# Second matmul in seven block products, x cast in DRAM and turned by DMA, row checks moved: a gated MLP on one Trainium2 core

## The chip, the core and the metric

The kernel runs on one core of one Trainium2 chip. The metric is device time in microseconds (us), so less is better. A time is the median of several executions; a profile is one execution taken by the hardware profiler, and its span is 1.6 to 1.9 us shorter than the time of that execution. PE is the tensor engine (TensorE), PEld its weight load, DVE VectorE, ACT ScalarE, POOL GpSimd, SP SyncE.

## The reference

```python
batch, seq, dim, hidden = 16, 256, 512, 2048
x:  [16, 256, 512]   w1: [512, 4096]   w2: [2048, 512]      # float32, normal draws
h = x @ w1
gate, value = np.split(h, 2, axis=-1)
h = np.maximum(gate, 0) * value
return (h @ w2).astype(np.float32)
```

## The kernel before

The 4096 rows of x are four superblocks (s = 0 to 3 in the code, one to four in the text) of 1024 rows. In each, a first matmul makes 16 hidden blocks of 128 columns, by a Strassen-Winograd scheme: the 2x2 block product of (two row halves of x) x (two halves of the contraction) with (gate, value) takes seven products P1 to P7 in place of eight, on sums of x (S1 to S4) and of w1 (T1 to T4) that are made beforehand. Each product here is two matmuls of 512 columns. Then the second matmul, h times w2, is done plainly.

```python
SLOT = {"P1": 0, "P5": 1, "P2": 3, "P6": 4, "P3": 5, "P7": 9, "P4": 13}   # in steps; a block has a period of 7

class Block:                                    # one hidden block of the first matmul
    def P1(self):
        self.X = psx.tile(...); self.mm("P1", self.X, True)
        self.Y = psy.tile(...); nc.scalar.copy(out=self.Y, in_=self.X)          # ScalarE, PSUM to PSUM
    def P5(self):
        self.W = psw.tile(...); self.mm("P5", self.W, True)
        nc.scalar.activation(self.p5, self.W, COPY, scale=GS)                   # ScalarE
    def P2(self):
        self.mm("P2", self.X, False)            # adds to X: must wait for the copy of X to Y
    def P6(self):
        self.mm("P6", self.Y, False)
        nc.scalar.activation(self.u2, self.Y, COPY, scale=GS)                   # ScalarE
    def P3(self): ...                           # two VectorE instructions
    def P7(self): ...                           # one
    def P4(self): ...                           # one: writes the second half of g

def mm2_stream(s, g):                           # the second matmul: 8 x 16 matmuls of 512 columns
    for b in range(NB):
        ps = psx.tile([P, DO], F32, name="O", tag="X")
        for hc in range(NJ):
            nc.tensor.matmul(ps, g[:, hc, b * P:(b + 1) * P], w2_sb[:, hc, :], start=hc == 0, stop=hc == NJ - 1)
            ...
        nc.scalar.activation(o, ps, COPY, scale=1 / GS)                         # ScalarE evicts
        nc.sync.dma_start(out=out_v[s, b], in_=o)

def look_whole(t, at, of, half=False):          # a row check: sum of squares, on ScalarE
    nc.scalar.activation(sq[:, :of], t, SQUARE, scale=..., accum_out=st[:, at:at + 1])

# which block of which superblock gets a check behind its P6
LOOKS = {(1, i): lambda i=i: look_w1(i) for i in range(16)}
LOOKS.update({(0, 8 + i): lambda i=i: look_first(i) for i in range(8)})
LOOKS.update({(2, i): lambda i=i: look_w2(i) for i in range(8)})
```

The checks decide on the device whether the inputs fit the scaled fp16 way; if not, a general fallback runs. x is loaded in 32-row strips, cast by ScalarE and transposed by VectorE during the second matmul. Each engine works through its own instructions in order.

## Time and profile before

| | before |
|---|---|
| time, median (range) | 336.24 us (336.1 to 336.59, 4 runs) |
| span of the profile, granted clock | 334.7 us, 0.997 |
| superblocks one to four | 72.3, 79.7, 78.3, 77.7 us |
| start to the first block / last matmul to the end | 20.8 / 5.9 us |

A superblock is timed here from its first block's first matmul to that of the next superblock, read in the PE timeline. Below are, from the page of the kernel before, the busy time of each engine and the busy tenths of PE and ACT in 40 equal slices of the span.

```profile
PE 321.7 (96%) x1475; PEld 145.0 (43%) x1475; DVE 199.5 (60%) x307; ACT 180.6 (54%) x332; POOL 113.1 (34%) x142
PE   8979999999999999999999999999999999999992
ACT  2568798832267878764128785554215555541120
```

PE is busy 96%, so it sets the time; but a busy PE can still be stretched. The timeline of the kernel before shows what a matmul costs. Columns are start, length, engine, line, operation, output and inputs, shape and count; in brackets is idle time and its releaser.

```profile
6.75 1.69 PE L148 MATMUL X<-warm 128*128 128x256 f16 x14
...
99.15 0.60 ACT L242 ACTIVATE pu<-Y 128x512 f32<-128x512 f32 x1 [0.59 <-PE Y L221]
99.64 1.05 ACT L173 ACTIVATE sq<-w_B_88 128x1024 f16<-128x1024 f16 x1
99.81 0.59 PE L221 MATMUL X<-x_A_782,w_B_88 128*128 128x512 f16 x2
100.59 0.19 ACT L173 ACTIVATION_READ_ACCUMULATOR sq<-w_B_88 128x1 f32 x1
100.68 0.59 PE L221 MATMUL Y<-x_S_788,w_T_93 128*128 128x512 f16 x2
100.68 0.59 ACT L228 COPY Y<-X 128x512 f32<-128x512 f32 x1
101.32 0.59 PE L221 MATMUL X<-x_A_783,w_B_89 128*128 128x512 f16 x2
```

The warm-up line prices a 256-column matmul, weight load included: 14 take 1.69 us and the last lasts 272 ns, so they start (1.69 - 0.272) / 13 = 0.109 us apart. The other lines are one block of superblock two. Products start 0.43 us apart, so P2, on w_B_89, should start at 101.11. It starts at 101.32, because it must wait for the copy of X to Y (L228), which began at 100.68 although its X, P1 of 99.81, was complete some 0.3 us before. ScalarE was still in the row check (L173) and its read-out. I call such a delay a hole: the step from one matmul's start to the next, less 0.2158 us (512 columns) or 0.1092 us (256). Superblock two has holes of 3.7 us in all, three of 2.2, one of 3.0 (1.5 and 0.64 of them in its first two blocks), four none to speak of.

### The profile page before, as it was taken

The page shows a single profiled execution, that of the slowest core. Times are in us where ns is not written, and L with a number is a line of the kernel's source. Part 1 is how long each engine was busy: PE and PEld are TensorE (multiplying, and loading weights), DVE is VectorE, ACT ScalarE, POOL GpSimd, SP SyncE. Part 2 cuts the span into 40 slices and gives each one's busy share as a digit, 9 for nine tenths or more (in the row PEclk, how much of TensorE's full clock was granted, in tenths as well). Part 3 has the DMA queues.
Part 4 walks back from the last instruction along what each step waited for, and adds up shares of the span by engine and source line. Part 5 has one row for each costly group of instructions (what it writes and reads, how often), then busy time and mean ns, then how long its engine had stood idle before and what let it go on. Part 6 is the DMA issues. An engine that isn't in the chain of part 4 may idle for free. (4 is left out here: it accounts for less than half of the span.)

```text
span 334.7 us, 4222 instructions
## 1 busy us (share of the span) xinstructions
PE 321.7 (96%) x1475; PEld 145.0 (43%) x1475; DVE 199.5 (60%) x307; ACT 180.6 (54%) x332; POOL 113.1 (34%) x142
## 2 busy tenths in 40 slices
PE   8979999999999999999999999999999999999992
PEld 4634444444444444444443444444444444444441
DVE  0477888866038778775207788885805888882000
ACT  2568798832267878764128785554215555541120
POOL 1679979299800000038950000019970000000000
PEclk9999999999999999999999999999999999999998
DMA  8946599942126000004116300004120000000212
GB/s 252 358 144 182 195 238 161 169 113 78 63 90 163 1 0 0 2 1 158 65 63 162 58 2 0 0 2 125 63 96 31 1 1 2 0 0 33 94 65 69
DMA packets 30458, 27.59 MB, mean 82 GB/s; under 512 B 1632, under 2 KB 25440, under 8 KB 30432
## 3 DMA queue, kind: packets, MB, share of 16 engines
q1 hardware_dynamic: 27136, 24.52, 24.8%
q0 software_dynamic: 2112, 2.10, 3.9%
q10 hardware_dynamic: 1184, 0.66, 0.6%
q8 instruction: 13, 0.21, 0.3%
q14 instruction: 13, 0.11, 0.1%
HBM read 20.97 MB, written 8.39 MB: 88 GB/s over the span
## 5 line engine op out<-in xcount | busy, mean ns | idle before, releaser
L286 PE MATMUL O<-w_sb,g 128*128 128x512 f16 x512 | 113.4, 379 | 0.0
L248 DVE SCALAR_TENSOR_TENSOR cc<-W,pu 128x512 f32<-128x512 f32 x62 | 42.9, 692 | 73.3 <-ACT pu L242 73.2
L286 PEld LDWEIGHTS <-g 128*128 128x128 f16 x512 | 50.1, 98 | 60.5 <-issue 0.2
L164 POOL TENSOR_TENSOR fold<-xh 128x1024 f32<-128x1024 f16 x12 | 24.0, 1999 | 114.0 <-ACT xh L186 113.3
L298 ACT ACTIVATE o<-O 128x512 f32<-128x512 f32 x31 | 18.5, 597 | 69.1 <-PE O L286 65.3
L242 ACT ACTIVATE pu<-Y 128x512 f32<-128x512 f32 x62 | 37.0, 597 | 33.6 <-PE Y L221 32.7
L228 ACT COPY Y<-X 128x512 f32<-128x512 f32 x62 | 35.9, 578 | 25.1 <-PE X L221 17.9
L249 DVE SCALAR_TENSOR_TENSOR g<-X,cc 128x512 f16<-128x512 f32 x62 | 42.9, 692 | 2.3
L258 DVE SCALAR_TENSOR_TENSOR g<-Y,cc 128x512 f16<-128x512 f32 x62 | 42.3, 681 | 2.7 <-PE Y L221 2.7
L167 POOL TENSOR_TENSOR fold<-fold 128x512 f32<-128x512 f32 (+2 forms) x72 | 41.3, 574 | 5.6
L254 DVE SCALAR_TENSOR_TENSOR cc<-Y,pu 128x512 f32<-128x512 f32 x62 | 42.3, 682 | 0.1
L235 ACT ACTIVATE pu<-W 128x512 f32<-128x512 f32 x62 | 37.1, 598 | 0.0
L221 PEld LDWEIGHTS <-w_B_89 128*128 128x128 f16 x124 | 12.1, 97 | 23.3 <-issue 12.0
L221 PEld LDWEIGHTS <-w_T_94 128*128 128x128 f16 x124 | 12.1, 97 | 15.8 <-issue 3.5
L221 PEld LDWEIGHTS <-w_T_93 128*128 128x128 f16 x124 | 12.1, 98 | 14.6
L221 PEld LDWEIGHTS <-w_T_91 128*128 128x128 f16 x124 | 12.1, 98 | 14.6
L221 PEld LDWEIGHTS <-w_B_88 128*128 128x128 f16 x124 | 12.0, 97 | 14.7
L221 PEld LDWEIGHTS <-w_T_92 128*128 128x128 f16 x124 | 12.0, 97 | 14.7
L221 PEld LDWEIGHTS <-w_B_90 128*128 128x128 f16 x124 | 12.0, 98 | 14.4
L295 DVE TENSOR_SCALAR o<-O 128x256 f32<-128x256 f32 x1 | 0.4, 425 | 25.3 <-ACT o L293 25.3
L186 ACT CAST xh<-xs 128x1024 f16<-128x1024 f32 x12 | 12.2, 1042 | 5.4 <-DMA xs<-in_x_dram 5.4
L203 POOL TENSOR_TENSOR w_T_91<-w_stage 128x512 f16<-128x512 f32 x7 | 9.2, 1313 | 7.5 <-DMA w_stage<-in_w_dram 7.3
(155 smaller groups left out, 429.9 us busy)
## 6 DMA issues: line engine op xcount, KB each, us to landing
out_dram<-o SPq DMA_DIRECT2D x31, 256.0 KB, 2.0
w_stage<-in_w_dram SPq DMA_DIRECT2D x7, 1024.0 KB, 6.9
xs<-in_x_dram SPq DMA_DIRECT2D x48, 128.0 KB, 3.9
w_sb<-in_w_dram POOLq DMA_DIRECT2D x4, 512.0 KB, 8.6
w_stage<-in_w_dram ACTq DMA_DIRECT2D x1, 512.0 KB, 5.3
w_stage<-in_w_dram SPq DMA_DIRECT2D x1, 512.0 KB, 6.6
x_A_162<-in_x_dram SPq DMA_DIRECT2D x1, 256.0 KB, 2.8
x_A_163<-in_x_dram SPq DMA_DIRECT2D x1, 256.0 KB, 4.1
```

Source lines behind the costliest of these rows:

```text
L164: nc.gpsimd.tensor_tensor(fold, t, t, op=MULT)
L167: nc.gpsimd.tensor_tensor(fold[:, :, :m], fold[:, :, :m], fold[:, :, m:2 * m], op=ADD)
L221: nc.tensor.matmul(ps, wop[wn][:, b, self.jb * P:(self.jb + 1) * P], self.xo[xn][:, b, :], start=fresh and b == 0, stop=b == 1, skip_group ...
L228: nc.scalar.copy(out=self.Y, in_=self.X)
L235: nc.scalar.activation(self.p5, self.W, COPY, scale=GS)
L242: nc.scalar.activation(self.u2, self.Y, COPY, scale=GS)
L248: nc.vector.scalar_tensor_tensor(out=self.c12, in0=self.W, scalar=GS, in1=self.u2, op0=MULT, op1=ADD)
L249: nc.vector.scalar_tensor_tensor(out=self.g[:, self.jb, :TH], in0=self.X, scalar=0.0, in1=self.c12, op0=MAX, op1=MULT)
L254: nc.vector.scalar_tensor_tensor(out=self.c22, in0=self.Y, scalar=GS, in1=self.p5, op0=MULT, op1=ADD)
L258: nc.vector.scalar_tensor_tensor(out=self.g[:, self.jb, TH:], in0=self.Y, scalar=0.0, in1=self.c22, op0=MAX, op1=MULT)
L286: nc.tensor.matmul(ps, g[:, hc, b * P:(b + 1) * P], w2_sb[:, hc, :], start=hc == 0, stop=hc == NJ - 1)
L298: nc.scalar.activation(o, ps, COPY, scale=1 / GS)
```

## The change

Its intent: the second matmul goes through the same seven products, on 128-row pairs of tokens with 256 output columns, so 7/8 of the work. To free ScalarE and VectorE for it, x of later superblocks is cast to fp16 by a DMA from DRAM to DRAM, turned by DMA transposes, and the sums of x for superblocks three and four go to GpSimd in the first matmul (those for superblock two stay on VectorE, the checks of later x on GpSimd as before). The checks of w1 and w2 move into the second matmul. One more difference is not in the cut below: each load of w1 for two blocks, 1 MB before, is now two of 512 KB. The diff, cut to its core:

```diff
-    w2_sb = wpool.tile([P, NJ, DO], F16, name="w2_sb")
+    vop = {n: wpool.tile([P, NJ // 2, DO // 2], F16, name=f"v_{n}") for n in ("B11", "B21", "B22", "T1", ... "T4")}
-    def turn_x(o, t, i): ...          # ScalarE cast, VectorE transposes
+    def cast_x(s):
+        x16[s] = dram.tile([2 * TH, D], F16, name="x16")
+        nc.gpsimd.dma_start(out=x16[s], in_=x2[s * 2 * TH:(s + 1) * 2 * TH, :])
+    def load_x(s, o):
+        for h in range(2):
+            for e in range(4):
+                nc.sync.dma_start(out=o[f"A{h + 1}{e // 2 + 1}"][:, e % 2],
+                                  in_=x16[s][h * TH:(h + 1) * TH, e * P:(e + 1) * P], transpose=True)
...
-    def mm2_stream(s, g): ...
+    class Pair:                       # 7 products of 8 matmuls with 256 columns
+        def P1(self): ... nc.scalar.copy(out=self.Y, in_=self.X)
+        def P5(self): nc.scalar.activation(self.pu[:, 0], self.W, COPY, scale=1 / GS); some_look()
+        def P2(self): nc.scalar.activation(self.o[:, 0, :DO // 2], self.X, COPY, scale=1 / GS)
+        def P6(self): nc.scalar.activation(self.pu[:, 1], self.Y, COPY, scale=1 / GS); some_look()
+        def P3(self): nc.vector.scalar_tensor_tensor(...)      # W + pu[1]
+        def P7(self): nc.vector.scalar_tensor_tensor(...)      # Y + pu[0]
+        def P4(self): nc.scalar.activation(...)
+    ORDER = ("P1 0, P1 1, P2 0, P2 1, P5 0, P6 0, P3 0, P7 0, P5 1, P4 0, P6 1, P3 1, P7 1, P1 2, P4 1, P5 2, P2 2, "
+             "P6 2, P3 2, P7 2, P1 3, P4 2, P5 3, P2 3, P6 3, P3 3, P7 3, P4 3")
...
-    LOOKS = {(1, i): lambda i=i: look_w1(i) for i in range(16)}
-    LOOKS.update({(0, 8 + i): lambda i=i: look_first(i) for i in range(8)})
-    LOOKS.update({(2, i): lambda i=i: look_w2(i) for i in range(8)})
+    LOOKS = {(0, 2 + i): lambda i=i: look_first(i) for i in range(8)}
+    LOOK_JOBS = [... look_w1(i), 16 ...] + [... look_w2(i), 8 ...]     # taken by some_look, 8 in each of s = 0, 1, 2
+    CASTS = {(0, 7): 1, (0, 13): 2, (1, 3): 3}                         # (superblock, block): which x is cast
+    SUMS_AT = (10, 11, 12, 13), (22, 26, 34, 38), (46, 53, 57, 61), (70, 78, 82, 87)   # VectorE, S1 S2 S4 S3 of each pair
...
+                    elif todo == len(wl):                              # at block 12 of superblock one
+                        for n2, i0, i1 in (("T1", "T3", "B11"), ("T2", "B22", "T1")):
+                            nc.gpsimd.tensor_tensor(vop[n2], vop[i0], vop[i1], op=SUB)
+                    if 4 <= todo < 8:                                  # a quarter of w2, cast as it is loaded
+                        nc.gpsimd.dma_start(out=vop[n2], in_=w2_v[...])
+        if s == 0:
+            job(20, lambda: nc.vector.tensor_tensor(vop["T3"], vop["B22"], vop["T3"], op=SUB))
+            job(30, lambda: nc.vector.tensor_tensor(vop["T4"], vop["B21"], vop["T2"], op=SUB))
```

"P7 0" is product P7 of pair 0; the text calls the pairs first to fourth. A product has four steps of two matmuls, and a job at step n is recorded on its engine just before that step's matmuls.

More of the change, by code (lines that the diff above doesn't have):

```diff
@@ L116, in fast_way @@
     gpool = ctx.enter_context(tc.tile_pool(name="gpool", bufs=1))
-    stage = ctx.enter_context(tc.tile_pool(name="stage", bufs=3))
+    dram = ctx.enter_context(tc.tile_pool(name="dram", bufs=NS - 1, space=bass.MemoryType.DRAM))
     halfs = ctx.enter_context(tc.tile_pool(name="halfs", bufs=4))
@@ L122, in fast_way @@
     psw = ctx.enter_context(tc.tile_pool(name="psw", bufs=2, space=bass.MemoryType.PSUM))
-    x_v = x2.rearrange("(s h tb r) (q c) -> s h q r tb c", h=2, tb=16, r=32, q=4)
-    w1_v = w1.rearrange("(p e) (g j) -> p (e g) j", e=4, g=2)
-    w2_v = w2.rearrange("(hc p) n -> p hc n", p=P)
-    out_v = out2.rearrange("(s b p) n -> s b p n", p=P, b=NB)
+    w1_v = w1.rearrange("(e p) (g j) -> g p e j", p=P, g=2)
+    w2_v = w2.rearrange("(u hc p) (v n) -> u v p hc n", u=2, v=2, p=P)
+    out_v = out2.rearrange("(s h b p) n -> s h b p n", p=P, h=2, b=NB // 2)
     wop = {n: wpool.tile([P, 2, H], F16, name=f"w_{n}") for n in ("B11", "B21", "B22", "T1", "T2", "T3", "T4")}
-    w2_sb = wpool.tile([P, NJ, DO], F16, name="w2_sb")
+    vop = {n: wpool.tile([P, NJ // 2, DO // 2], F16, name=f"v_{n}") for n in ("B11", "B21", "B22", "T1", "T2", "T3", "T4")}
     w_stage = wpool.tile([P, 4, 1024], F32, name="w_stage")
@@ L151, in x_tiles, with sums_of @@
     def x_tiles():
-        return {n: xpool.tile([P, 2, TH], F16, name=f"x_{n}", tag=f"x_{n}")
-                for n in ("A11", "A12", "A21", "A22", "S1", "S2", "S3", "S4")}
-    def x_sums(o):
+        o = {n: xpool.tile([P, 2, TH], F16, name=f"x_{n}", tag=f"x_{n}")
+             for n in ("A11", "A12", "A22", "S1", "S2", "S3", "S4")}
+        o["A21"] = o["S3"]
+        return o
+    def sums_of(o, eng=nc.vector):
         for n, i0, i1, op in (("S1", "A21", "A22", ADD), ("S2", "S1", "A11", SUB), ("S4", "A12", "S2", SUB),
                               ("S3", "A11", "A21", SUB)):
-            yield nc.vector.tensor_tensor(o[n], o[i0], o[i1], op=op)
+            yield eng.tensor_tensor(o[n], o[i0], o[i1], op=op)
     def look(t, at):
@@ L174, in look_whole, with load_rows @@
                              accum_out=st[:, at:at + 1])
-    def load_x(s, i):
-        t = stage.tile([P, 8, P], F32, name="xs", tag="xs")
-        for q in range(4):
-            nc.sync.dma_start(out=t[q * 32:(q + 1) * 32], in_=x_v[s, i // 2, q, :, i % 2 * 8:i % 2 * 8 + 8])
-        return t
-    def turn_x(o, t, i):
-        ts = slice(i % 2 * 256, i % 2 * 256 + 256)
-        c = halfs.tile([P, 8, P], F16, name="xh", tag="xh")
-        nc.scalar.copy(out=c, in_=t)
-        halves.append(c)
-        for k in range(2):
-            nc.vector.transpose(o[f"A{i // 2 + 1}{k + 1}"][:, :, ts].rearrange("p b (tb r) -> p b tb r", r=32),
-                                c.rearrange("p tb (c k b) -> p k b tb c", k=2, b=2)[:, k])
+    x16 = {}
+    def cast_x(s):
[6 more added lines that the diff above has]
+                                  in_=x16[s][h * TH:(h + 1) * TH, e * P:(e + 1) * P], transpose=True)
+    def load_rows(s, i):
+        t = halfs.tile([P, 8, P], F16, name="xh", tag="xh")
+        nc.sync.dma_start(out=t.rearrange("p (b q) c -> p b (q c)", b=2),
+                          in_=x16[s][i * 2 * P:(i + 1) * 2 * P].rearrange("(b p) d -> p b d", p=P))
+        return t
     def load_w1(eng, jb, n, u):
-        t = w_stage[:, u:u + n].rearrange("p u v -> p (u v)").rearrange("p (eg j) -> p eg j", eg=8)
-        eng.dma_start(out=t, in_=w1_v[:, :, jb * P:(jb + n) * P])
-        return t.rearrange("p (k b g) j -> p k b g j", k=2, b=2)
+        t = w_stage[:, u:u + n].rearrange("p u v -> p (u v)").rearrange("p (g e j) -> p g e j", g=2, e=4)
+        for v in range(2):
+            eng.dma_start(out=t[:, v], in_=w1_v[v, :, :, jb * P:(jb + n) * P])
+        return t.rearrange("p g (k b) j -> p k b g j", k=2)
     def w1_ops(jb, n, t):
@@ L279, in products @@
                                            in1=v, op0=MAX, op1=MULT)
-    def mm2_stream(s, g):
-        last = s == NS - 1
-        for b in range(NB):
-            ps = psx.tile([P, DO], F32, name="O", tag="X")
-            for hc in range(NJ):
-                nc.tensor.matmul(ps, g[:, hc, b * P:(b + 1) * P], w2_sb[:, hc, :],
-                                 start=hc == 0, stop=hc == NJ - 1)
-                if hc < NJ - 1:
-                    yield
-            o = tmp.tile([P, DO], F32, name="o", tag="tmp")
-            if last and b == NB - 1:
-                h = DO // 2
-                nc.scalar.activation(o[:, :h], ps[:, :h], COPY, scale=1 / GS)
-                nc.scalar.dma_start(out=out_v[s, b, :, :h], in_=o[:, :h])
-                nc.vector.tensor_scalar(out=o[:, h:], in0=ps[:, h:], scalar1=1 / GS, scalar2=None, op0=MULT)
-                nc.sync.dma_start(out=out_v[s, b, :, h:], in_=o[:, h:])
-            else:
-                nc.scalar.activation(o, ps, COPY, scale=1 / GS)
-                nc.sync.dma_start(out=out_v[s, b], in_=o)
-            yield
@@ L302, in advance, with __init__, product, send @@
-    def advance(stream, n):
+    s_place = w_stage.rearrange("p u v -> p (u v)").bitcast(F16).rearrange("p (i n h t) -> p i n h t", i=2, n=4, t=P)
+    class Pair:
+        def __init__(self, s, g, t):
+            self.s, self.t = s, t
+            self.end = s == NS - 1 and t == NB // 2 - 1
+            o = {f"A{h + 1}{u + 1}": g[:, u * NJ // 2:(u + 1) * NJ // 2, h * TH + t * P:h * TH + (t + 1) * P]
+                 for h in range(2) for u in range(2)}
+            o.update({f"S{n + 1}": s_place[:, t % 2, n] for n in range(4)})
+            self.op = o
+        def product(self, name):
+            c = slice(0, DO // 2)
+            if name == "P1":
+                self.X = psx.tile([P, TH], F32, name="X", tag="X")[:, c]
+            elif name == "P5":
+                self.W = psw.tile([P, TH], F32, name="W", tag="W")[:, c]
+            ps = self.X if name in ("P1", "P2") else self.W if name in ("P5", "P3") else self.Y
+            wn, an = WX[name]
+            for i in range(NJ // 2):
+                nc.tensor.matmul(ps, self.op[an][:, i], vop[wn][:, i], start=name in ("P1", "P5") and i == 0,
+                                 stop=i == NJ // 2 - 1, skip_group_check=True)
+                if i == NJ // 2 - 1:
+                    getattr(self, name)()
+                if i % 2:
+                    yield
+        def send(self, h, c):
+            nc.sync.dma_start(out=out_v[self.s, h, self.t, :, c], in_=self.o[:, h, c])
+        def P1(self):
+            self.Y = psy.tile([P, TH], F32, name="Y", tag="Y")[:, :DO // 2]
+            nc.scalar.copy(out=self.Y, in_=self.X)
+        def P5(self):
+            self.pu = tmp.tile([P, 2, DO // 2], F32, name="pu2", tag="tmp")
+            nc.scalar.activation(self.pu[:, 0], self.W, COPY, scale=1 / GS)
+            some_look()
+        def P2(self):
+            self.o = tmp.tile([P, 2, DO], F32, name="o", tag="tmp")
+            nc.scalar.activation(self.o[:, 0, :DO // 2], self.X, COPY, scale=1 / GS)
+        def P6(self):
+            nc.scalar.activation(self.pu[:, 1], self.Y, COPY, scale=1 / GS)
+            some_look()
+        def P3(self):
+            nc.vector.scalar_tensor_tensor(out=self.o[:, 0, DO // 2:], in0=self.W, scalar=1 / GS, in1=self.pu[:, 1],
+                                           op0=MULT, op1=ADD)
+            self.send(0, slice(0, DO))
+        def P7(self):
+            nc.vector.scalar_tensor_tensor(out=self.o[:, 1, DO // 2:], in0=self.Y, scalar=1 / GS, in1=self.pu[:, 0],
+                                           op0=MULT, op1=ADD)
+            if self.end:
+                self.send(1, slice(DO // 2, DO))
+        def P4(self):
+            nc.scalar.activation(self.o[:, 1, :DO // 2], self.Y, COPY, scale=1 / GS)
+            self.send(1, slice(0, DO // 2 if self.end else DO))
@@ new lines, in fast_way, with mm2_stream @@
+    ORDER = ("P1 0, P1 1, P2 0, P2 1, P5 0, P6 0, P3 0, P7 0, P5 1, P4 0, P6 1, P3 1, P7 1, P1 2, P4 1, P5 2, P2 2, "
+             "P6 2, P3 2, P7 2, P1 3, P4 2, P5 3, P2 3, P6 3, P3 3, P7 3, P4 3")
+    LAST_ORDER = ORDER.replace("P1 3, P4 2, P5 3, P2 3, P6 3, P3 3, P7 3", "P1 3, P5 3, P2 3, P6 3, P4 2, P7 3, P3 3")
+    def mm2_stream(s, pairs):
+        for step in (LAST_ORDER if s == NS - 1 else ORDER).split(", "):
+            name, t = step.split()
+            yield from pairs[int(t)].product(name)
@@ L303, in advance @@
+    stream_at = {}
+    def advance(stream, n, todo={}):
         for _ in range(n):
-            if stream is None or next(stream, 0) == 0:
+            if stream is None:
                 return
+            at = stream_at[stream] = stream_at.get(stream, -1) + 1
+            for job in todo.get(at, ()):
+                job()
+            next(stream, 0)
     wl = [(0, 1, 0), (1, 1, 1)] + [(jb, 2, jb % 4) for jb in range(2, NJ, 2)]
@@ L345, in fast_way @@
     x_nat = x2.rearrange("(s h b p) d -> s h b p d", h=2, b=4, p=P)
-    place = list(x_tiles().values())
-    xn = [[t.rearrange("p b t -> p (b t)").bitcast(F32) for t in place[4 * h:4 * h + 4]] for h in range(2)]
+    place = [*x_tiles().values()][:7] + [halfs.tile([P, 8, P], F16, name="xh", tag="xh")]
+    xn = [[t.rearrange("p a b -> p (a b)").bitcast(F32) for t in place[4 * h:4 * h + 4]] for h in range(2)]
     def fetch_first(h):
@@ L357, in turn_first @@
             for e in range(4):
-                nc.tensor.transpose(ps[:, e * P:(e + 1) * P], xn[h][b].rearrange("p (c e) -> p e c", e=4)[:, e], ident)
+                nc.tensor.transpose(ps[:, e * P:(e + 1) * P], xn[h][b][:, e * P:(e + 1) * P], ident)
             for k, copy in ((0, nc.vector.tensor_copy), (1, nc.scalar.copy)):
@@ L383, in fast_way @@
     prepare(3)
-    sums = x_sums(xo)
+    sums = sums_of(xo)
     next(sums)
@@ L392, in fast_way, with some_look @@
     copy_some(2)
-    halves, LOOKX = [], {}
+    LOOKX, looks = {}, []
+    def some_look():
+        if looks:
+            looks.pop(0)()
     def look_x(s, i):
-        look(halves[i], 32 * s - 24 + 8 * i)
-        if i == 3:
-            halves.clear()
+        look(load_rows(s, i), 32 * s - 24 + 8 * i)
     def look_w1(i):
@@ L408, in look_w2 @@
     def look_w2(i):
-        look_whole(w2_sb[:, 2 * i:2 * i + 2].rearrange("p h n -> p (h n)"), NX + 16 + i, 1024)
+        n = ("B11", "B21", "B22", "T1")[i // 2]
+        look_whole(vop[n].rearrange("p (u h) n -> p u (h n)", u=2)[:, i % 2], NX + 16 + i, 1024, n == "T1")
     def judge():
@@ L428, in fast_way @@
         LOOKX.update({(s, 2 * i): (s, i) for i in range(4)})
-    LOOKS = {(1, i): lambda i=i: look_w1(i) for i in range(16)}
-    LOOKS.update({(0, 8 + i): lambda i=i: look_first(i) for i in range(8)})
-    LOOKS.update({(2, i): lambda i=i: look_w2(i) for i in range(8)})
+    LOOKS = {(0, 2 + i): lambda i=i: look_first(i) for i in range(8)}
+    LOOK_JOBS = [lambda i=i: look_w1(i) for i in range(16)] + [lambda i=i: look_w2(i) for i in range(8)]
     LOOKS[3, 10] = judge
@@ L436, in fast_way @@
     TAIL = 4
+    CASTS = {(0, 7): 1, (0, 13): 2, (1, 3): 3}
+    SUMS = (9, 10, 11, 12)
+    SUMS_AT = (10, 11, 12, 13), (22, 26, 34, 38), (46, 53, 57, 61), (70, 78, 82, 87)
     for s in range(NS):
@@ L444, in fast_way @@
         stream = None
-        if s + 1 < NS:
-            xs = []
         last = NJ * PERIOD
@@ L450, in fast_way @@
             if at == last - 7:
-                stream = mm2_stream(s, g)
+                pairs = [Pair(s, g, t) for t in range(NB // 2)]
+                stream = mm2_stream(s, pairs)
             if at in plan:
@@ L459, in fast_way @@
                     elif todo == len(wl):
-                        for h0 in (0, 4, 8, 12):
-                            nc.gpsimd.dma_start(out=w2_sb[:, h0:h0 + 4, :], in_=w2_v[:, h0:h0 + 4, :])
+                        for n2, i0, i1 in (("T1", "T3", "B11"), ("T2", "B22", "T1")):
+                            nc.gpsimd.tensor_tensor(vop[n2], vop[i0], vop[i1], op=SUB)
                         for j in range(0, NPLAIN, 2):
                             plain_w_end(j, 2)
-                if n == "P1" and jb in (9, 11, 13) and s + 1 < NS:
-                    xs.append(load_x(s + 1, len(xs)))
+                    if 4 <= todo < 8:
+                        n2 = ("B11", "T3", "B22", "B21")[todo - 4]
+                        nc.gpsimd.dma_start(out=vop[n2], in_=w2_v[(0, 0, 1, 1)[todo - 4], (0, 1, 1, 0)[todo - 4]])
+                if n == "P1" and jb == (10 if s == 0 else 1) and s + 1 < NS:
+                    xo_next = x_tiles()
+                    load_x(s + 1, xo_next)
+                if n == "P1" and (s, jb) in CASTS:
+                    cast_x(CASTS[s, jb])
+                if s and n == "P3" and jb in SUMS and s + 1 < NS:
+                    if jb == SUMS[0]:
+                        sums = sums_of(xo_next, nc.gpsimd)
+                    next(sums)
                 getattr(blocks[jb], n)()
@@ L476, in fast_way, with job @@
                 advance(prev, 2)
-        if s + 1 < NS:
-            xo = x_tiles()
-            turn_x(xo, xs[0], 0)
-            advance(stream, 6)
-            turn_x(xo, xs[1], 1)
-            xs.append(load_x(s + 1, 3))
-            advance(stream, 12)
-            turn_x(xo, xs[2], 2)
-            advance(stream, 18)
-            turn_x(xo, xs[3], 3)
-            for _ in x_sums(xo):
-                pass
-            advance(stream, NB * NJ - TAIL - 46)
+        jobs = {}
+        def job(at, *what):
+            jobs.setdefault(at, []).extend(what)
+        for t, at in enumerate(SUMS_AT):
+            sums = sums_of(pairs[t].op)
+            for u in at:
+                job(u, lambda sums=sums: next(sums))
+        if s == 0:
+            job(20, lambda: nc.vector.tensor_tensor(vop["T3"], vop["B22"], vop["T3"], op=SUB))
+            job(30, lambda: nc.vector.tensor_tensor(vop["T4"], vop["B21"], vop["T2"], op=SUB))
+        if s + 1 < NS:
+            xo = xo_next
+            if s == 0:
+                sums = sums_of(xo)
+                for u in (84, 90, 93, 96):
+                    job(u, lambda sums=sums: next(sums))
+            looks = [lambda i=i: LOOK_JOBS[i]() for i in range(8 * s, 8 * s + 8)]
+            advance(stream, 112 - TAIL - 10, jobs)
         else:
@@ L492, in fast_way @@
                                    skip_runtime_bounds_check_because="a comparison wrote it")
-            advance(stream, NB * NJ)
+            advance(stream, 112, jobs)
         prev = stream
```

## The prediction

> **What bounds the kernel now.** TensorE. The page gives PE 96% of the 334.7 us span, and a granted clock of 0.997. In the timeline two 512-column matmuls start every 0.431 us: 215.8 ns each; 900 of the first matmul and 512 of the second make 304.7 us. The rest is start (first real matmul at 11.0 us), end (6 us after the last matmul), and holes. In the PE timeline, start to start beyond the nominal step, I count 3.0 us in superblock one's first matmul (1.5 and 0.64 in its first two blocks), 3.7 us in superblock two, 2.2 in three. The last two are regular: 0.21 us per block, always before the product that needs X copied to Y, and only where ScalarE also does a 128x1024 row check of w1 or w2 (1.05 + 0.19 us): ScalarE is the slower engine there. Superblock four has neither.
>
> **What the change removes.**
> 1. The second matmul goes from 128 matmuls of 512 columns to 224 of 256 per superblock. The trace prices them: the 14 warm-up matmuls 128x256, each with its weight load, take 1.69 us in the timeline, the last 272 ns, so 109 ns start to start. This agrees with the Trainium skill, "TensorE: Matmul & The Clock Gate", Back-to-back issue gap (N/2.4 + 2.5 ns). 224 x 0.1092 = 24.5 us against 27.6: 12.6 us in all, on the critical path.
> 2. The w1 and w2 checks move from ScalarE in the first matmul into the second, where it is 30% busy: 5.9 us of holes go.
> 3. ScalarE's casts (12.2 us) and VectorE's transposes (16 us) of x leave; they were hidden, but make room for the sums.
>
> **What it adds.**
> - 64 VectorE sums of 128x1024 fp16, 0.69 us each where GpSimd is quiet: 11 us per 24.5 us stage, hidden except the first: after the last block's g write (0.6 us) S1 needs 0.69, and only 1.3 us of products stand between: 0.25 us per stage.
> - ScalarE checks between evictions: P7 of the first pair waits for P6's eviction behind a check, 0.2 us per stage; output buffers in a rotation of four: some tenths more.
> - Superblock one: x checks move onto blocks 2 to 9, where weight casts also load ScalarE (+0.6 us); w2 loads (4 MB, cast) run beside the w1 loads, whose landing (6.9 us) has about 2 us of room: 0 to 4 us, 1.5 expected; T3 on VectorE delays P7 0, 0.3 us.
> - DRAM casts and DMA transposes: off the path. GpSimd sums and checks within the first matmul: free, as VectorE's PSUM operations kept 0.69 us beside GpSimd's weight sums.
>
> Sum: 336.3 - 12.6 - 5.9 + 4.2 = 322.
>
> **Predicted: 322 us, range 318.5 to 327.5. Faster by over 2%: 0.94; within 2%: 0.05; slower: 0.01.**
>
> **What would show each step.** Second-matmul stages of 24.5 to 25.5 us; no 0.21 us holes in superblocks two and three; superblock one's holes at 3 to 7 us, ended by ScalarE or a w1 DMA; second-matmul holes ended by VectorE sums (before P5 of pair 0) and ScalarE evictions. Start and end unchanged within 0.5 us.
>
> **What would make it wrong.** 256-column matmuls not hiding real weight loads; w2 or cast traffic starving w1; GpSimd slowing VectorE's fp16 sums (up to 2.4 us beside GpSimd in this trace); DMA transposes so slow that superblock two starts late; ScalarE blocked on output buffers, rippling into the products.

## The result, and the profile after

The changed kernel takes 325.21 us (322.68 to 325.93, 4 runs) against 336.24 us. The ratio is 0.9657 (0.9604 to 0.9709): faster. A ratio here is the mean time of one kernel's fast runs over that of the other's in the same rounds, so not quite the ratio of the medians quoted.

The prediction's range held it, 3.2 us above the 322 predicted. The kernel before keeps within about half a microsecond in those runs; the changed one spreads over 3.2 us. In the longest later series, 11 runs of the kernel before spread over 1.75 us and 6 of the changed one over 3.1. Page of the changed kernel:

```profile
PE 307.2 (95%) x1859; PEld 181.6 (56%) x1859; DVE 229.0 (71%) x372; ACT 181.3 (56%) x368; POOL 135.6 (42%) x155
PE   8979998997999999999999999999999999999992
ACT  2569996435665555545766555545665555552230
```

Next, busy time of each engine by superblock, before and then after. Columns: window, length, busy us (instructions started) of PE, PEld, DVE, ACT, POOL, then the granted clock, DMA share and GB/s.

```profile
20.78:93.07 72.29, 70.09 (x321) 31.23 (x320) 49.13 (x72) 45.47 (x87) 57.70 (x62) 1.00 0.63 153
93.07:172.74 79.67, 78.42 (x354) 34.30 (x353) 49.13 (x76) 50.83 (x92) 22.89 (x32) 1.00 0.18 54
172.74:251.05 78.31, 77.41 (x353) 34.34 (x352) 52.19 (x76) 43.13 (x76) 22.81 (x32) 1.00 0.19 54
251.05:328.79 77.74, 77.74 (x358) 34.63 (x356) 42.13 (x69) 31.62 (x56) 0.00 (x0) 1.00 0.08 28
```

```profile
20.82:95.04 74.22, 67.89 (x414) 40.02 (x412) 57.35 (x89) 52.28 (x111) 44.64 (x34) 1.00 0.69 155
95.04:168.73 73.69, 73.40 (x450) 43.62 (x448) 54.69 (x88) 42.32 (x84) 30.29 (x37) 1.00 0.26 72
168.73:242.42 73.69, 73.40 (x450) 43.61 (x448) 54.70 (x88) 42.33 (x84) 29.77 (x36) 1.00 0.19 58
242.42:317.18 74.76, 74.62 (x459) 44.34 (x456) 55.80 (x94) 34.47 (x68) 21.33 (x32) 1.00 0.13 45
```

Superblock two is 5.98 us shorter, three 4.62, four 2.98. Superblock four had no checks before and prepares no later x, so its gain is that of the seven products: 3.16 us on paper, less a hole of 0.30. The other two add their checks' holes. But superblock one became 1.9 us longer: PE is busy 67.9 of 74.2 us there, and its holes went from 3.0 to 8.1 us. Holes in the changed kernel's PE timeline, as I count them:

| where | us | predicted |
|---|---|---|
| one, first matmul, blocks 2 and 3 (there before: 2.14) | 2.23 | as before |
| one, blocks 4 to 9, before P2, ScalarE casts and x checks (there before: 0.88, in part other blocks) | 1.14 | +0.6 |
| one, blocks 11 and 12 | 2.17 | 1.5 (w1 loads) |
| one, second matmul, before P5 of the first pair | 0.60 | 0.25 |
| one, before P7 of the first pair | 0.62 | 0.5 |
| one, before P4 of the first pair | 1.36 | none |
| two and three, before P5 of the first pair | 0.37 and 0.36 | 0.25 each |
| two and three, before P7 of the first pair | 0.25 and 0.25 | 0.2 each |
| four, before P5 of the first pair | 0.30 | 0.25 |

The hole at blocks 11 and 12, in the timeline of the changed kernel (superblock one, end of the w1 loads):

```profile
54.07 0.60 PE L230 MATMUL W<-x_S_196,w_T_90 128*128 128x512 f16 x2
54.65 0.62 ACT L216 CAST w_B_89<-w_stage 128x512 f16<-128x512 f32 x1 [2.31 <-DMA w_stage<-in_w_dram]
54.77 1.25 POOL L212 TENSOR_TENSOR w_T_90<-w_stage 128x512 f16<-128x512 f32 x1 [4.99 <-DMA w_stage<-in_w_dram]
55.17 0.59 ACT L251 ACTIVATE pu<-Y 128x512 f32<-128x512 f32 x1
55.81 0.59 PE L230 MATMUL Y<-x_S_198,w_T_92 128*128 128x512 f16 x2 [1.14 <-ACT pu L251]
```

The DMA times of the w1 loads, from the kernel's instructions on their staging tile, before and then after:

```profile
DMA to landing us min/median/max: 5.3/6.6/8.9
```

```profile
DMA to landing us min/median/max: 3.8/5.7/13.1
```

ScalarE and GpSimd wait 2.31 and 4.99 us for the last piece of w1. ScalarE's cast of that piece stands in order before the eviction of Y (L251), and P7 waits for that: PE stands still. The slowest w1 load, of 512 KB, took 13.1 us to land; before, of 1 MB, it was 8.9.

The hole before P4 of the first pair, in the same kernel's timeline:

```profile
77.08 1.04 PE L312 MATMUL W<-v_T_97,w_stage 128*128 128x256 f16 x8
77.39 0.42 DVE L340 SCALAR_TENSOR_TENSOR o<-W,pu_845 128x256 f32<-128x256 f32 x1
77.72 1.22 DVE L571 TENSOR_TENSOR v_T_100<-v_B_95,v_T_98 128x2048 f16<-128x2048 f16 x1
78.86 0.41 DVE L345 SCALAR_TENSOR_TENSOR o<-Y,pu_845 128x256 f32<-128x256 f32 x1
79.32 0.93 PE L312 MATMUL Y<-v_T_100,g 128*128 128x256 f16 x7 [1.20 <-DVE o L345]
```

P5 of the second pair starts at 77.08, and P4 of the first should follow at 77.95. P4 adds to Y, which VectorE must first have read for P7 (L345). VectorE does so at 78.86 only: T4 (L571), 128x2048, was placed one step ahead of it. P4 also multiplies by T4, so it needs both. From 72.03 until both are done VectorE is never idle for more than 0.1 us: it has too much to do before P4.

### The profile page after: what moved, and what is told of

The parts are those of the page before. It is cut to its first block, busy times and chain, and to the rows that moved or that the text cites. A ratio compares the mean times of both kernels' runs of the same rounds, so it can differ in the third digit from the quotient of the medians.

```text
span 323.5 us, 5169 instructions
## 1 busy us (share of the span) xinstructions
PE 307.2 (95%) x1859; PEld 181.6 (56%) x1859; DVE 229.0 (71%) x372; ACT 181.3 (56%) x368; POOL 135.6 (42%) x155
## 4 chain that ended last, share of the span: by engine, by line
PE 86%; DVE 5%; ACT 5%; issue 2%; DVEq 0%; ACTq 0%
PE Y L230 24%; PE X L230 16%; PE W L230 15%; PE Y L312 12%; PE W L312 7%; PE X L312 7%; PE Y L148 2%; DVE w_stage L161 2%; ACT sq L176 1%; PE X L283 1%; PE W L283 1%; DVE g L267 1%; ACT Y L237 1%; ACT w_B_88 L216 1%; DVE x_A_193 L428 1%
## 5 line engine op out<-in xcount | busy, mean ns | idle before, releaser
L167 POOL TENSOR_TENSOR fold<-xh 128x1024 f32<-128x1024 f16 x12 | 22.7, 1894 | 107.9 <-DMA xh<-x_704 40.9
L251 ACT ACTIVATE pu<-Y 128x512 f32<-128x512 f32 x62 | 37.0, 597 | 34.6 <-PE Y L230 33.8
L312 PEld LDWEIGHTS <-w_stage 128*128 128x128 f16 x512 | 49.7, 98 | 9.0 <-DVE w_stage L161 2.1
L312 PEld LDWEIGHTS <-g 128*128 128x128 f16 x384 | 37.5, 98 | 9.7 <-issue 1.6
L170 POOL TENSOR_TENSOR fold<-fold 128x512 f32<-128x512 f32 (+2 forms) x72 | 38.8, 539 | 5.6
L161 DVE TENSOR_TENSOR w_stage<-g 128x1024 f16<-128x1024 f16 x32 | 21.2, 690 | 0.2
L312 PE MATMUL Y<-v_T_100,g 128*128 128x256 f16 x128 | 17.1, 272 | 1.2 <-DVE o L345 1.2
L312 PE MATMUL W<-v_T_97,w_stage 128*128 128x256 f16 x128 | 16.6, 273 | 1.0 <-DVE w_stage L161 0.8
L312 PE MATMUL Y<-v_T_99,w_stage 128*128 128x256 f16 x128 | 16.6, 273 | 0.6 <-DVE v_T_99 L570 0.5
```

What stands on the lines that cost most here:

```text
L161: yield eng.tensor_tensor(o[n], o[i0], o[i1], op=op)
L167: nc.gpsimd.tensor_tensor(fold, t, t, op=MULT)
L170: nc.gpsimd.tensor_tensor(fold[:, :, :m], fold[:, :, :m], fold[:, :, m:2 * m], op=ADD)
L312: nc.tensor.matmul(ps, self.op[an][:, i], vop[wn][:, i], start=name in ("P1", "P5") and i == 0, stop=i == NJ // 2 - 1, skip_group_check=True)
```

## The experiments

Ten kernels ran, all with correct results, against runs of the kernel before on the same chip (335.4 to 337.2 us). The series were taken on three chips; the kernel before had medians of 336.12, 336.25 and 336.25 us there, so times are compared across them. Their lengths of superblocks and holes are read in the PE timelines as above.

### 1. The changed kernel again

No edit.

> The changed kernel once more, unedited: a base for the other runs and a look at its own spread (322.7 to 325.9 us so far, where the kernel before keeps within 0.5 us). Theory 'cast': superblock one has a hole of about 2.2 us at blocks 11 and 12, where ScalarE and GpSimd wait for the last w1 load, and whether that load loses the race against the DRAM cast of x differs from run to run; so runs lie from 322.5 to 326 us. Rival 'w2': the four cast loads of w2 share the DMA engines with w1 and always slow it by the same; then the hole is there in every run and the spread has another source. Expected median 324.5 to 325.5.

Measured: 325.36 us (322.87 to 325.95, 6 runs), ratio 0.967. One run of six took 322.9 us, as one of the first four took 322.7; the others lie near 325. The profiled run was one of the longer ones; the hole at blocks 11 and 12 was there with 1.07 us, and its size thus differs between runs (2.17 in the first profile). Experiments 4 to 7 leave the program up to there as it is, and give four more profiles. Ordered by the landing of the slowest w1 load, 10.5, 10.6, 12.3, 12.5, 12.7 and 13.1 us, the six have holes of 0, 0.26, 1.31, 1.53, 1.07 and 2.17 us.

### 2. The first cast of x later

```diff
-    CASTS = {(0, 7): 1, (0, 13): 2, (1, 3): 3}
+    CASTS = {(0, 11): 1, (0, 13): 2, (1, 3): 3}
-                if n == "P1" and jb == (10 if s == 0 else 1) and s + 1 < NS:     # load_x: the DMA transposes
+                if n == "P1" and jb == (12 if s == 0 else 1) and s + 1 < NS:
```

> The first DRAM cast of x is issued at block 11 instead of 7, which in GpSimd's order is after the last w1 load has landed; its DMA transposes start at block 12 and have until the end of the stage. Theory 'cast': the wait for the last w1 load at blocks 11 and 12 goes, 1.5 to 2.2 us less than the unedited run's median, 322.5 to 323.3, and the spread of the runs falls to about 1 us. Rival 'w2': the hole stays, time within 0.5 us of the unedited run. If the transposes then come too late, a new hole stands at the start of superblock two or before the sums of x on VectorE late in stage one.

Measured: 323.11 us (322.13 to 324.18, 5 runs), ratio 0.9621 (0.9597 to 0.9644). The hole is gone, superblock one is 71.9 us long, and the slowest w1 load lands in 9.1 us. The four loads of w2 were untouched, so the rival falls. The hole was absent in one profile with the cast in its place too, so the time counts here more than the one profile; and the transposes moved with the cast, which experiment 3 leaves alone. The spread only fell to 2 us: part of it is elsewhere (the first block starts between 20.4 and 21.7 us in the profiles of kernels with the same start).

### 3. The casts cut into rows, in their places

```diff
-        nc.gpsimd.dma_start(out=x16[s], in_=x2[s * 2 * TH:(s + 1) * 2 * TH, :])
+        rows = "(b p) d -> p b d"
+        nc.gpsimd.dma_start(out=x16[s].rearrange(rows, p=P),
+                            in_=x2[s * 2 * TH:(s + 1) * 2 * TH, :].rearrange(rows, p=P))
```

> The casts keep their places, but each is cut into 1024 rows of 2 KB read and 1 KB written, spread over 128 outer steps[...]. Theory 'cast by large packets': the w1 load's last packets and its semaphore no longer stand behind packets of 16 to 32 KB, so the wait at blocks 11 and 12 falls from 2.3 us to under 1 us although the same bytes move at the same time; time 322.5 to 324. Rival 'bytes': what matters is that 3 MB more move beside the load, whatever the packet size; then the hole stays at 1.5 to 2.5 us and the time within 0.5 us of the unedited run. Rival 'w2': no change either.

Measured: 322.83 us (321.96 to 323.72, 4 runs), ratio 0.9598 (0.9577 to 0.9619). The hole is gone though the same bytes move at the same time. Windows of two us, first the changed kernel, whose last w1 load lands at 54.62, then the one with rows, where it lands at 50.11 (columns as above):

```profile
50.00:52.00 2.00, 2.00 (x11) 0.90 (x10) 1.55 (x4) 1.77 (x4) 0.00 (x0) 1.00 1.02 217
52.00:54.00 2.00, 2.00 (x11) 0.89 (x10) 1.16 (x2) 0.33 (x1) 0.00 (x0) 1.00 0.39 83
```

```profile
50.00:52.00 2.00, 2.00 (x10) 0.87 (x9) 1.56 (x3) 1.64 (x4) 1.74 (x3) 1.00 1.26 209
52.00:54.00 2.00, 2.00 (x11) 0.93 (x10) 1.55 (x4) 1.74 (x4) 2.00 (x3) 1.00 1.24 208
```

Its w1 loads:

```profile
DMA to landing us min/median/max: 3.9/5.7/8.3
```

In the changed kernel GpSimd does nothing in these 4 us and ScalarE almost nothing in the last two. The DMA figures need care: these windows count a packet where it starts, with its whole length. Spread over the time that the packets take, the records give 217 and 216 GB/s and a DMA share of 1.01 in both windows, so the engines were full, and the bytes moved as fast as with rows (207 and 209, counted in the same way).

What differs is how the end of the load fits in. The cast has 32 packets of 32 KB and 2.43 us: 16 start from 49.0 to 50.3, as many as there are engines, the other 16 from 51.4 to 52.7, each as one of the first ends. Of the w1 load's queue 2 data packets (1 KB and 0.06 us) were left at 49.45. They start at 51.67 and 51.76, between the two rounds, and two packets of 4 bytes, the last before the landing, at 54.14 and 54.23, as the second round ends. So the last of the load waits one or two packets of 2.43 us. The landings agree: where the queue is through between the rounds, the load lands at 52.1 and 52.2 us (the profiles with holes of 0 and 0.26), otherwise at 54.3 to 54.6.

With rows of 1 KB the load lands in 8.3 us at worst, and GpSimd goes on working. The Trainium skill, "DMA: Bandwidth & Descriptors", Queues, rings and completion order, says that each DMA engine takes turns between queues packet by packet. That fits these times. The packet records don't say which engine a packet is on, so they don't show the turns of one engine by themselves.

### 4. T4 on GpSimd

```diff
-                        for n2, i0, i1 in (("T1", "T3", "B11"), ("T2", "B22", "T1")):
+                        for n2, i0, i1 in (("T1", "T3", "B11"), ("T2", "B22", "T1"), ("T4", "B21", "T2")):
-            job(30, lambda: nc.vector.tensor_tensor(vop["T4"], vop["B21"], vop["T2"], op=SUB))
```

> The sum T4 of w2 (128x2048) is made by GpSimd straight after T2 instead of by VectorE at step 30 of the first second matmul. Theory 'T4': the 1.36 us hole before the first pair's P4 is P4 waiting for VectorE's read of Y, which stands behind T4 in VectorE's order; it goes, and the time falls by 1.2 to 1.4 us. Rival 'contention': GpSimd, now busy 4 us longer, slows the first fp16 sums on VectorE (0.87 us and more in place of 0.69), and the hole before the first pair's P5 grows from 0.60 us by as much as is won; time within 0.5 us of the unedited run.

Measured: 327.85 us (324.84 to 328.61, 6 runs), ratio 0.9769: 2.5 us slower than the unedited kernel. The hole before P4 fell to 0.24 us, but those before P5, P6, P3 and P7 of the first pair became 1.35, 0.68, 0.68 and 0.85. VectorE and GpSimd in its timeline:

```profile
70.65 1.62 DVE L161 TENSOR_TENSOR w_stage<-g 128x1024 f16<-128x1024 f16 x1
71.69 1.60 POOL L408 TENSOR_TENSOR w_T<-w_B,w_T 128x512 f16<-128x512 f16 x1
72.37 1.47 DVE L161 TENSOR_TENSOR w_stage<-w_stage,g 128x1024 f16<-128x1024 f16 x1
73.25 1.60 POOL L409 TENSOR_TENSOR w_T<-w_B,w_T 128x512 f16<-128x512 f16 x1
73.87 1.53 DVE L161 TENSOR_TENSOR w_stage<-g,w_stage 128x1024 f16<-128x1024 f16 x1
75.32 0.68 DVE L161 TENSOR_TENSOR w_stage<-g 128x1024 f16<-128x1024 f16 x1
```

VectorE's fp16 sums took 1.47 to 1.62 us in place of 0.69 while GpSimd worked on its own sums, which are pushed 4 us later by T4, and the sum at 75.32, after GpSimd's last, took 0.68 again. The rival was right, and stronger than I had it. The Trainium skill, "SBUF — State Buffer", Who interferes with whom, says that a VectorE instruction with two SBUF inputs contends with a GpSimd instruction that reads SBUF, and one with at most one SBUF input, outside the two-port modes, does not. This agrees on both: VectorE's operations on PSUM in the first matmul kept 0.69 us beside GpSimd's weight sums. All these holes together are 1.2 us more than the unedited kernel's in the same place; its profiled run took 326.08 us, where four of the six took 327.8 to 328.6. That profile has no hole at blocks 11 and 12, where the unedited kernel's have 1.07 and 2.17; the longer runs probably had one, which would make up most of the rest, but no profile of them shows it.

### 5. T4 after the read, on VectorE

```diff
-            job(30, lambda: nc.vector.tensor_tensor(vop["T4"], ...
+            job(32, lambda: nc.vector.tensor_tensor(vop["T4"], ...
-    ORDER = ("... P7 0, P5 1, P4 0, P6 1, P3 1, ...
+    ORDER = ("... P7 0, P5 1, P6 1, P4 0, P3 1, ...
```

> T4 stays on VectorE but comes after VectorE's read of Y for P7 of the first pair, and P4 of the first pair comes one product later, behind P6 of the second. GpSimd is not touched. Theory 'T4 before the read': the 1.36 us hole before P4 of the first pair falls under 0.2 us, the time by 1.1 to 1.4 us against the unedited 325.3 us, that is 324.0 us. Rival: P4 waits for T4 itself wherever it stands, or for ScalarE; then a hole of 0.5 us or more stays before P4, P3 or P7 of the first two pairs.

Measured: 324.63 us (321.71 to 324.98, 4 runs), ratio 0.9631 (0.9581 to 0.9681). In the profile the hole fell from 1.36 to 0.49, not under 0.2. From its timeline:

```profile
76.81 1.04 PE L312 MATMUL W<-v_T,w_stage 128*128 128x256 f16 x8
77.45 0.41 DVE L345 SCALAR_TENSOR_TENSOR o<-Y,pu 128x256 f32<-128x256 f32 x1
77.78 1.22 DVE L571 TENSOR_TENSOR v_T<-v_B,v_T 128x2048 f16<-128x2048 f16 x1
79.05 1.03 PE L312 MATMUL Y<-v_T,g 128*128 128x256 f16 x8 [0.33 <-DVE v_T L571]
```

VectorE read Y at 77.45, made T4 from 77.78, and P4 waited for T4 itself, as the rival had it. The edit changed two things, and they can be told apart here: P4 starts 2.24 us after P5 of the second pair (76.81), and in the unedited kernel 2.24 as well (79.32 after 77.08). So the exchange of T4 and the read gained nothing, since P4 needs both; the 0.87 us is the one product that now stands before P4 (8 times 0.1092). The theory was wrong about the order, and the hole is the time that VectorE needs for both. The median fell by 0.7 us against experiment 1, with overlapping intervals.

### 6. More products before the first use of S1

```diff
-    ORDER = ("P1 0, P1 1, P2 0, P2 1, P5 0, P6 0, P3 0, P7 0, P5 1, P4 0, P6 1, P3 1, P7 1, P1 2, P4 1, P5 2, P2 2, "
+    ORDER = ("P1 0, P1 1, P2 0, P2 1, P1 2, P5 0, P6 0, P3 0, P7 0, P5 1, P4 0, P6 1, P3 1, P7 1, P5 2, P4 1, P2 2, "
```

> P1 of the third pair is put before P5 of the first, so that 0.87 us more of products stand between the last block's g write and the first use of S1. Theory 'S1': the holes before P5 of the first pair (0.60 us in superblock one, 0.36 us in two and three, 0.30 in four) go, 1.6 us in all, and the rest stays: 323.7 us beside an unedited 325.3. T3's hole in superblock one (0.62 us) may shrink too, by up to 0.4 us, as P7 of the first pair comes no earlier while T3 does not move. Rival: those holes belong to other evictions or to PSUM buffers, and the earlier P1, which takes the third buffers of X and Y, makes a new hole of the same size.

Measured: 322.10 us (321.96 to 323.08, 4 runs), ratio 0.9591 (0.9568 to 0.9615). The holes before P5 of the first pair are gone in all four superblocks; two, three and four are 73.34, 73.35 and 74.45 us, 0.3 to 0.35 less each. T3's hole shrank from 0.62 to 0.36, and P4's grew to 1.97. That explains 1.3 us of the 3.2 won. In the profiled run the rest is the hole at blocks 11 and 12, 0.26 us here; the times of the other three suggest the same, but they have no profile. The program is the same up to there; its load came through between the cast's two rounds (experiment 3), and what decides that no run shows.

### 7. One part undone: checks back in the first matmul

```diff
+    for i in range(24):
+        LOOKS[(1, i) if i < 16 else (2, i - 16)] = LOOK_JOBS[i]
-            looks = [lambda i=i: LOOK_JOBS[i]() for i in range(8 * s, 8 * s + 8)]
```

> The changed kernel with that part alone undone: w1 and w2 checks back behind P6 of the blocks of superblocks two and three. Theory 'checks': the 0.21 us holes come back (24 of them, 5.9 us with the two larger first ones), and the 0.25 us hole before P7 of the first pair goes in superblocks two and three, since it is P6's eviction behind a check; 325.3 + 5.4 = 330.7 us (329.5 to 331.5). What is then left of the gain over 336.1, about 5.4 us, belongs to the seven products and the x path, of 12.6 us that the products save on paper.

Measured: 329.38 us (326.44 to 330.36, 4 runs), ratio 0.9783 (0.9724 to 0.9842), whether over 2% faster than the kernel before is unclear. The 0.21 us holes are back, one per block with a check, 0.48 in the first; those before P7 of the first pair are gone in superblocks two and three, which are 76.63 and 75.30 us long, 2.94 and 1.61 more. That is 4.55 us where I expected 5.4; the first block's hole of 0.48 in place of 0.70 is 0.4 of it.

### 8. One part alone: the kernel before, its checks moved

```diff
-    LOOKS = {(1, i): lambda i=i: look_w1(i) for i in range(16)}
-    LOOKS.update({(2, i): lambda i=i: look_w2(i) for i in range(8)})
+    LOOKS = {}
+    LOOK_JOBS = [lambda i=i: look_w1(i) for i in range(16)] + [lambda i=i: look_w2(i) for i in range(8)]
                 nc.scalar.activation(o, ps, COPY, scale=1 / GS)          # in mm2_stream
                 nc.sync.dma_start(out=out_v[s, b], in_=o)
+                if s < NS - 1:
+                    LOOK_JOBS[8 * s + b]()
```

> The kernel before, with one part of the change alone: its 24 ScalarE row checks of w1 and w2 (128x1024) stand behind the output evictions of the second matmul, eight in each of the first three superblocks, instead of behind P6 of the first matmul's blocks. Theory 'checks': the holes of 0.21 us a block in superblocks two and three are ScalarE's and go; 336.1 - 5.9 = 330.2 us, superblocks two and three 76 us long instead of 79.7 and 78.3, with no new holes, as ScalarE has over 60% of the second matmul free. Rival 'elsewhere': the holes have another cause, for instance the DVE or the weight loads, and the superblocks keep their lengths.

Measured: 334.40 us (333.78 to 335.12, 4 runs), ratio 0.9952 (0.9927 to 0.9978): a third of what I expected. The regular holes are gone, but superblocks two, three and four each have a new one of 1.08 us in their first block. The timeline of superblock two:

```profile
95.96 0.60 ACT L298 ACTIVATE o<-O 128x512 f32<-128x512 f32 x1 [0.27 <-PE O L286]
96.45 1.05 ACT L173 ACTIVATE sq<-w_B 128x1024 f16<-128x1024 f16 x1
97.49 0.59 ACT L228 COPY Y<-X 128x512 f32<-128x512 f32 x1
98.13 0.59 PE L221 MATMUL X<-x_A,w_B 128*128 128x512 f16 x2 [0.91 <-ACT Y L228]
```

The last output block is evicted (L298) within the next superblock's first block, and my check stood right behind it, ahead of the copy of X to Y (L228). The same edit with no check behind the last two evictions:

```diff
+                    for i in {0: (0,), 1: (1,), 2: (2,), 3: (3,), 4: (4, 5), 5: (6, 7)}.get(b, ()):
+                        LOOK_JOBS[8 * s + i]()
```

> The kernel before with its w1 and w2 checks in the second matmul as in the earlier run, but none behind the last two output evictions, which run within the next superblock's first blocks. Theory: the 1.08 us hole at the start of superblocks two to four of that run was the copy of X to Y standing behind the eviction and check of the last output block; it goes, and the full 5.9 us of the checks is gained: 336.2 - 5.9 = 330.3 us (329.5 to 331.5). Rival: the hole has another cause (VectorE's sums of x, the first block itself), and the time stays at 334.

Measured: 330.91 us (330.55 to 331.33, 4 runs), ratio 0.9836 (0.9819 to 0.9853), superblocks 72.6, 76.3, 76.3 and 77.7 us, with no holes above 0.1 us in the last three. The hole had the cause that was named. So half of the change's gain, 5.3 of 11.0 us, is to be had from the place of 24 checks, with no new product.

### 9. All repairs together

Beside edits 2, 3 and 6:

```diff
-    LOOKS = {(0, 2 + i): lambda i=i: look_first(i) for i in range(8)}
+    LOOKS = {(0, jb): lambda i=i: look_first(i) for i, jb in enumerate((3, 5, 7, 9, 11, 12, 13, 14))}
+    # x transposes of superblock two from block 15; P4 0 behind P6 1; T4 on GpSimd straight after T2
+    # the four sums for the two plain blocks (plain_w_end): from GpSimd to VectorE, steps 40, 44, 65, 74
+    # the first pair's check behind P4 in place of P5; the last output half sent from ScalarE's queue
```

> The changed kernel with all repairs: first cast of x at block 11 and all casts cut into rows; x transposes from block 15; the checks of x on blocks 3, 5, 7, 9, 11 to 14, so never on a block with two weight casts; P1 of the third pair before P5 of the first; the first pair's check behind P4 instead of P5; T4 on GpSimd straight after T2, early enough to be over when the fp16 sums begin, and the four sums for the plain blocks moved from GpSimd to VectorE in the second matmul to make that room; the last output half sent from ScalarE's queue. If the holes found so far are independent, superblock one is 71.87 (cast late) - 0.42 - 0.62 - 1.37 - 1.14 = 68.3 us, two and three 73.70 - 0.36 - 0.25 = 73.1, four 74.4, and the time about 318 us (316.5 to 319.5) with a spread under 2 us. Rival: the repairs are not independent; GpSimd's T4 now meets VectorE's sums as in the earlier run, or the transposes come too late for the sums of x, and 1 to 3 us of new holes stand in superblock one.

Measured: 317.48 us (316.31 to 317.77, 5 runs), ratio 0.9425 (0.9404 to 0.9446). By superblock:

```profile
21.40:89.60 68.20, 66.71 (x413) 40.08 (x412) 57.36 (x92) 52.44 (x111) 43.82 (x31) 1.00 0.82 170
89.60:162.67 73.07, 73.07 (x451) 43.71 (x449) 54.50 (x88) 42.31 (x84) 30.64 (x37) 1.00 0.29 73
162.67:235.73 73.06, 73.06 (x450) 43.72 (x448) 54.50 (x88) 42.32 (x84) 29.77 (x36) 1.00 0.20 59
235.73:310.17 74.44, 74.44 (x459) 44.37 (x456) 55.60 (x94) 34.48 (x68) 21.32 (x32) 1.00 0.13 45
```

That is 68.2, 73.07, 73.06 and 74.44 us, where 68.3, 73.1, 73.1 and 74.4 were expected: the repairs add up, so they are independent as far as this profile shows. PE has no hole above 0.1 us in superblocks two to four. In this kernel T4 on GpSimd ended at 68.84 us and VectorE's first fp16 sum began at 69.00, and that sum took 0.69. T4 was no harm on GpSimd here, where it was over in time.

## Why the prediction was right or wrong, point by point

- **PE bounds the kernel, and 256-column matmuls cost 109 ns.** Right. Superblocks two without holes are 76.31 us with the plain second matmul (experiment 8, mended) and 73.07 with the seven products (experiment 9): 3.24 us, predicted 3.16.
- **The checks' holes, 5.9 us.** Right: 5.3 us from the move alone, and in the changed kernel no hole of 0.21 us is left in superblocks two and three. The reason given, "ScalarE is the slower engine there", is not: it was busy 82% there, and the check lay in a round of waits (see the profile before).
- **S1, "0.25 us per stage".** Right in mechanism (experiment 6), somewhat small: 0.30 to 0.37, and 0.60 in superblock one, where the first sum took 0.87 us beside GpSimd's last.
- **The check ahead of P6's eviction, "0.2 us per stage".** Right: 0.25, gone when the checks are taken out (experiment 7).
- **"Output buffers in a rotation of four: some tenths more".** Wrong: no PE hole was ended by them.
- **Superblock one, "+0.6 us" for the x checks.** Somewhat high: 1.14 in place of 0.88 us, and a tenth more in the first two blocks, 0.4 in all.
- **Superblock one, "w2 loads ... run beside the w1 loads ... 1.5 expected".** The size fits (0 to 2.17 us in six profiles), the cause does not, so the fit is luck. It was not w2 but the first DRAM cast of x, by its large packets (experiments 2 and 3). The prediction names cast traffic among what would make it wrong, but its "DRAM casts and DMA transposes: off the path" fails here: I looked at when the cast's result was needed, not at what it would collide with.
- **"T3 on VectorE delays P7 0, 0.3 us".** Right in mechanism, too small: 0.62, and it is T3's alone, which ended at 76.15 where the eviction behind the check was done at 75.78. And T4, ten steps later in the same list, was not costed at all; its 1.36 us is the largest miss. What was not added up is all that VectorE has to do before P4 of the first pair. With T4 on GpSimd the hole was 0.24 (experiment 4) and none (experiment 9).
- **GpSimd in the first matmul is free.** Right: no holes in the first matmul of superblocks two to four.
- **"Start and end unchanged within 0.5 us".** About right in the first profile: 20.82 against 20.78 us, and 6.32 against 5.87. In experiment 1, the same program, they were 21.66 and 6.70.

The sum of the additions was 4.2 us and came to about 7: T4 1.4, the w1 load 0.7 and S1 0.6 more than foreseen, the end 0.45, less the tenths for the buffers. That is the 3 us between 322 and 325. The path of x was never run alone: of its worth the runs show only what it cost here.

## What to carry to other kernels

Price an added instruction by all that its engine has to finish before the product that waits: a 1.2 us sum on a VectorE without pause cost the tensor engine 1.36 us. Exchanging it with a read that the same product needs gained nothing; one more product in front gained that product's 0.87 us, and with GpSimd making the sum, early enough not to slow VectorE, and P4 one product later too, the hole was gone (experiment 9). A transfer that is off the critical path can still hold up one that is on it; cut bulk copies into row-sized pieces, or issue them after the last critical load, and look at the slowest landing rather than the median. Before a rearrangement is bought, try its side moves alone: moving 24 checks gave half of this gain, and where they were put decided between 1.8 and 5.3 us.

## What the Trainium skill lacked or had wrong

- "TensorE: Matmul & The Clock Gate", Back-to-back issue gap, gives a sustained 131 ns per matmul of 512 columns for pairs of weight load and matmul. This case has a new weight load before each and takes 215.8 ns at 512 columns and 109.3 at 256 (8 in 0.874 us), which is the page's other formula, the one it calls isolated.
- "DMA: Bandwidth & Descriptors", Rules for kernel authors, advises transfers of 1 MiB and more for bandwidth and does not say what they do to others: beside a cast of 1 MB that moved in packets of 32 KB a 512 KB load landed in 13.1 us, against 8.3 at worst beside the same cast in rows of 1 KB; the kernel took 325.4 and 322.8 us.
- The same page, Latency and other measured facts, gives DMA transposes an effective 261 GB/s or more. Here eight transposes of 128x512 fp16 (1 MB) were issued over 10.3 us, 1.2 to 1.3 us each on SyncE's queue, and the DMA moved 105 GB/s from 58 to 66 us. The issues follow each other with less than 0.1 us between, so their length seems to be the limit; no run shows it, and the page has no time per issue for transposes of this size on this chip.
- "SBUF — State Buffer", Who interferes with whom, held in both directions: fp16 sums of two SBUF inputs 1.47 to 1.62 us in place of 0.69 beside GpSimd, operations with one PSUM input unchanged.
